# Low parts of 32 weight units by accumulating DMAs instead of VectorE

## The chip, the core and the metric

The kernel runs on one core of a Trainium2 chip. The metric is the device time of one execution in microseconds. The kernel before takes 855.59 us (median of 3 runs, 855.11 to 855.79).

The core has five engines with their own instruction queues, each worked off in order: TensorE (PE in the profile, with its weight loads as PEld), VectorE (DVE), ScalarE (ACT), GpSimd (POOL) and SyncE (SP). Sixteen DMA engines move data between memory and the on-chip SBUF.

## The reference

One decoder block on 512 tokens of width 1024, in float32. Two branches work on the same normed input and are merged by sigmoid gates; then come a squared-ReLU MLP of width 4096 and gated embeddings.

```
h = rms_norm(x, attn_norm_g);  u = h @ w_in                  # 1024 x 5376
u_sb, u_rw, u_gate = split(u)
o_sb = stick_breaking_attention(q, k, v of u_sb)             # 8 heads of 64
o_rw = rwkv7_time_mix(u_rw, ...)                             # 8 heads of 64, a recurrence over the tokens
g_sb, g_rw = sigmoid(u_gate)
x = x + (g_sb * (o_sb @ w_up_sb) + g_rw * (o_rw @ w_up_rw)) @ w_out
x = x + relu(rms_norm(x) @ w_ff1)**2 @ w_ff2
x = rms_norm(x + sigmoid(rms_norm(x) @ w_ple_gate) * (p @ w_ple_proj))
```

The recurrence of the RWKV branch, per head: S = S diag(w) + (S a) b^T + v k^T, y = S r.

## The kernel before

**Products in three parts.** TensorE multiplies in a format with a shorter mantissa (float32r). To keep float32's accuracy, every operand is split in a high part (the value rounded to float32r) and a low part (the value minus the high part), and a product is made of three matmuls: high by high (L244), low of the data by high of the weight (L245), high by low of the weight (L246). `mm3` issues the three; a weight unit is 128 x 1024 numbers (512 KB), eight `mm3` steps, 24 matmuls.

**Weight units.** All weights lie in memory as such units, and the list `seq` names them in the order of use: twelve of q, k and v, then (U_RW, 12) and (U_RW, 13), then the r, k and v projections of the four RWKV head pairs (U_RW, 0 to 11, three for each head pair), the gates (U_GSB and U_GRW, eight each), the two upward projections (U_UPSB and U_UPRW, four each), and the units of the later products. SyncE loads a unit to `w_raw` (L182, four buffers). `fetch_to` splits it: ScalarE casts it to `w_hi` (L225), VectorE writes `w_lo`, raw minus high (L227); `w_hi` and `w_lo` have three buffers each. `weights` hands a unit out. A unit's split is issued three `mm3` steps into the unit two places ahead of it, so it is to be ready some 1.6 units of matmuls later.

**Stages.** In the profile's time: to about 140 us the projections of q, k, v and the attention, with the last projections of that stage (among them (U_RW, 4), (U_RW, 0) and (U_RW, 8)) between its matmuls; from 140 to about 410 us the RWKV stage; then the merge and the product with `w_out`, then the MLP from about 480 us, and the gated embeddings at the end.

**The RWKV stage.** The four head pairs go through `prepare` and `scan`, one head pair's `scan` beside the next one's `prepare`. `prepare` builds operands for chunks of 64 tokens and inverts triangular matrices: on VectorE LM and DE (L852, L855), own (L888), the transposes LX (L899), tmp (L893), then seven pairs of X steps (L910, L911), own and X (L912, L915), with small matmuls on TensorE in between (L847, L901, L877, L937, L945, L956, L967). `scan` walks over the chunks: TensorE L996, VectorE UV (L998), TensorE L1005, VectorE S (L1013), which takes in Sg, made on GpSimd (L1012). Between these, as filling, stand the matmuls of the weight units above: their results leave PSUM by VectorE (u at L357, gg at L738). At the start of the stage ScalarE makes eight sigmoids (L682), a table load (L686), gx (L755) and further operands; GpSimd issues two accumulating DMAs (L635) which sum blocks of `w_out` to T3 and, after that has landed, T2.

**What sets the order.** The code is written as generators that `drive` interleaves, and a scheduler then sets the order of each engine's queue by its own reckoning of when each instruction can start; so a change of one instruction moves others. Waits are on semaphores. GpSimd issues the accumulating DMAs itself; one of them stands in its queue like any other instruction and waits there for its inputs.

Of the kernel before, what the change touches and what calls it, by code (L numbers as in the profile page):

```python
# [13 lines left out]
AF = mybir.ActivationFunctionType  # L14
ALU = mybir.AluOpType
# [25 lines left out]
U_PLE, U_QKV, U_RW, U_GSB, U_GRW, U_UPSB, U_UPRW, U_OUT, U_FF1, U_FF2, U_GATE = range(11)  # L41
# [52 lines left out]
def tile_block(ctx: ExitStack, tc: tile.TileContext, xT, xt, pT, wts, lora, cols_d, gfin_d, consts_d, out, dbg=None):  # L94
    nc = tc.nc
    act, dve, pool, pe, sync = nc.scalar, nc.vector, nc.gpsimd, nc.tensor, nc.sync
# [3 lines left out]
    def r32(ap):  # L100
        return ap.bitcast(F32)
# [34 lines left out]
    seq = []  # L136
# [24 lines left out]
    state = {"i": 0, "used": 0, "due": 0}  # L161
    AHEAD = 3
    homes = {}
# [3 lines left out]
    def unit(i):  # L167
        if seq[i][0] == U_FF2:
            return wts[UBASE[U_FF2] + seq[i][1] * 8 + FF2_FROM[seq[i][2]] + seq[i][3]]
        if seq[i][0] == U_S12:  # L170
            return wts[UBASE[U_FF1] + seq[i][1] * 8 + seq[i][2] + 4]
        if seq[i][1] == "s":
            return wts[UBASE[seq[i][0]] + FROM[seq[i][2]]]
        return wts[UBASE[seq[i][0]] + seq[i][1]]

    def load_to(n):
        while len(loaded) < min(n, len(seq)):
            i = len(loaded)
            loaded.append(None)
            if seq[i] not in sources and seq[i][0] not in (U_S3, U_S4):  # L180
                loaded[i] = wpool.tile([P, 1024], F32, name="w_raw", bufs=4)
                sync.dma_start(out=loaded[i], in_=unit(i))  # L182
                if seq[i][0] == U_FF2 and seq[i][2] == 3:
                    pool.dma_start(out=loaded[i], in_=wts[UBASE[U_FF2] + seq[i][1] * 8 + 4 + seq[i][3]], accum_op=ALU.add)
# [11 lines left out]
    def made(i):  # L196
        kind = seq[i][0]
        if seq[i] in sources:
            return sources[seq[i]]()
        if kind == U_S12:  # L200
            with tc.issue_after(state["wlo"]):
                four_sums(i)
            return sums12[seq[i][1:]][:, 0:2].rearrange("p s x -> p (s x)")
        if kind == U_S3:
            return loaded[i - 1]
        if kind == U_S4:
            return sums12.pop(seq[i][1:])[:, 2]
        return loaded[i]

    def fetch_to(n, ahead=0):  # L210
        while state["i"] < min(n, len(seq)):
            i = state["i"]
            state["i"] += 1
            load_to(i + 1 + ahead)
            raw = made(i)
            if seq[i] in homes:
                hi, lo = homes[seq[i]]()
            elif seq[i][0] == U_S4:
                hi = wpool.tile([P, 512], F32R, name="w_hi4", bufs=1)
                lo = wpool.tile([P, 512], F32R, name="w_lo4", bufs=1)  # L220
            else:
                hi = wpool.tile([P, 1024], F32R, name="w_hi")
                lo = wpool.tile([P, 1024], F32R, name="w_lo")
            with tc.issue_after(state["hx"] if seq[i] == (U_FF1, 4) else state["fourth"][0]) if seq[i] in ((U_FF1, 4), (U_OUT, 2), (U_OUT, 3)) else nullcontext():
                state["cast"] = act.copy(out=hi, in_=raw).ins  # L225
            with tc.issue_after(state["fourth"][1]) if seq[i] in homes and seq[i][0] == U_OUT else nullcontext():
                state["wlo"] = dve.tensor_tensor(out=lo, in0=raw, in1=r32(hi), op=ALU.subtract).ins  # L227
            if seq[i] == (U_OUT, "s", 4):
                state["fourth"] = state["cast"], state["wlo"]
            ready.setdefault(seq[i], []).append((hi, lo))  # L230

    def weights(*u):
        assert seq[state["used"]] == u, (seq[state["used"]], u)
        state["used"] += 1
        fetch_to(state["used"])
        state["due"] = 3
        return ready[u].pop(0)
# [11 lines left out]
    def step():  # L249
        state["due"] -= 1  # L250
        if state["due"] == 0:
            fetch_to(state["used"] + AHEAD - 1, 1)
# [77 lines left out]
    with ExitStack() as sA:  # L330
# [43 lines left out]
        with ExitStack() as s1:  # L374
# [47 lines left out]
            for i in range(2):  # L422
                ready[seq[i]] = [tuple(first_w[i])]
            fetch_to(3)

            for k in range(KT):
# [1262 lines left out]
```

## Time and profile before

| | |
|---|---|
| median of 3 runs | 855.59 us |
| profiled execution | 859.3 us, span 857.5 us |
| granted TensorE clock | 0.996 of full speed |
| busy: PE, DVE, ACT, POOL | 98%, 83%, 60%, 12% of the span |
| HBM read, written | 108.08 MB, 10.49 MB |

The span runs from the first to the last instruction of the profiled execution; its own device time is 1.8 us longer. "Busy" is the time in which an engine worked on an instruction. In rows of groups, `L227 DVE TENSOR_TENSOR w_lo<-w_raw,w_hi` is line 227 of the kernel before on VectorE, writing `w_lo` from `w_raw` and `w_hi`; after the shapes and the count stand the busy us, the mean ns of one, and the idle time of the engine ahead of them with what ended it. In rows of single instructions the start (us from the span's start) and the duration come first.

### The profile page before, as it was taken

Reading aid. Unit: us, or ns where it says so; the run is one execution under the profiler, and the core shown is the slowest. Engines: PE = TensorE matmul, PEld = TensorE weight load, DVE = VectorE, ACT = ScalarE, POOL = GpSimd, SP = SyncE. Lnnn points to the kernel's source line nnn. Section 1 sums busy time; section 2 is a strip of 40 time slices with the busy share of each in tenths; the row PEclk is TensorE's granted clock in tenths of the full one; section 3 lists DMA queues with packets and bytes.
Section 4 is the critical chain, followed back from the end, with each engine's and each line's share of the span. In section 5 each row is a group of like instructions: output and inputs, shape, how many; then the busy total and the mean of one; then the engine's idle time right before and its main releaser. Section 6 shows DMA issues by size and latency. Waiting matters only on the chain.

```text
span 857.5 us, 14647 instructions
## 1 busy us (share of the span) xinstructions
PE 840.8 (98%) x5594; PEld 697.5 (81%) x5594; DVE 712.6 (83%) x1264; ACT 513.1 (60%) x804; POOL 105.5 (12%) x174
## 2 busy tenths in 40 slices
PE   8999999999999999999999999999999999999996
PEld 5778788777777777777888888899889989988885
DVE  7989987896987969867896597899879988997767
ACT  7878887734436243533585575458647844783843
POOL 1332432001212101020000101000110010010000
PEclk9999999999999999999999999999999999999999
DMA  8311213421220323427882676973985489275402
GB/s 320 101 50 62 87 62 135 123 96 54 63 88 25 103 83 115 162 97 232 284 258 95 189 228 156 232 202 102 227 234 150 139 240 241 96 221 145 174 23 99
DMA packets 40197, 124.23 MB, mean 145 GB/s; under 512 B 4544, under 2 KB 4544, under 8 KB 40128
## 3 DMA queue, kind: packets, MB, share of 16 engines
q1 hardware_dynamic: 34944, 104.42, 35.7%
q0 software_dynamic: 5184, 18.88, 12.1%
q8 instruction: 44, 0.72, 0.4%
q14 instruction: 25, 0.20, 0.1%
HBM read 108.08 MB, written 10.49 MB: 138 GB/s over the span
## 4 chain that ended last, share of the span: by engine, by line
PE 87%; DVE 9%; issue 1%; ACT 1%; DMA 1%; SPq 0%; DVEq 0%; ACTq 0%
PE ps_m L244 14%; PE ps_m L245 14%; PE ps_m L246 14%; PE ps_m L260 9%; PE ps_m L259 9%; PE ps_m L261 9%; PE ps_g L877 1%; DVE w_lo L227 1%; PE ps_o L550 1%; PE ps_s L1005 1%; PE ps_z L558 1%; PE ps_c L996 1%; PE ps_g L967 1%; DVE LX L899 1%; DVE own L888 1%
## 5 line engine op out<-in xcount | busy, mean ns | idle before, releaser
L225 ACT CAST w_hi<-w_raw 128x1024 fp32r<-128x1024 f32 x122 | 128.0, 1051 | 122.4 <-PE ps_m L245 77.4
L227 DVE TENSOR_TENSOR w_lo<-w_raw,w_hi 128x1024 fp32r<-128x1024 f32 x122 | 149.0, 1224 | 24.2 <-ACT w_hi L225 23.5
L244 PE MATMUL ps_m<-h_hi,w_hi 128*128 128x512 f32 x320 | 130.6, 410 | 0.8 <-ACT w_hi L274 0.7
L246 PE MATMUL ps_m<-h_hi,w_lo 128*128 128x512 f32 x320 | 128.6, 402 | 0.0
L245 PE MATMUL ps_m<-h_lo,w_hi 128*128 128x512 f32 x320 | 128.2, 401 | 0.3 <-DVE h_lo L407 0.3
L244 PEld LDWEIGHTS ps_m<-h_hi,w_hi 128*128 128x128 f32 x320 | 60.7, 190 | 12.6 <-ACT w_hi L274 1.1
L246 PEld LDWEIGHTS ps_m<-h_hi,w_lo 128*128 128x128 f32 x320 | 60.4, 189 | 12.0
L245 PEld LDWEIGHTS ps_m<-h_lo,w_hi 128*128 128x128 f32 x320 | 60.5, 189 | 11.3 <-DVE h_lo L407 1.3
L245 PE MATMUL ps_m<-hx,w_hi 128*128 128x256 f32 (+1 forms) x208 | 65.8, 316 | 0.0
L244 PE MATMUL ps_m<-hx,w_hi 128*128 128x256 f32 (+1 forms) x208 | 65.8, 316 | 0.0
L246 PE MATMUL ps_m<-hx,w_lo 128*128 128x256 f32 (+1 forms) x208 | 65.7, 316 | 0.0
L244 PE MATMUL ps_m<-tb,w_hi 128*128 128x256 f32 x192 | 54.3, 283 | 0.0
L245 PE MATMUL ps_m<-tb,w_hi 128*128 128x256 f32 x192 | 54.3, 283 | 0.0
L246 PE MATMUL ps_m<-tb,w_lo 128*128 128x256 f32 x192 | 54.3, 283 | 0.0
L259 PE MATMUL ps_m<-w_hi,fS 128*128 128x512 f32 x128 | 49.8, 389 | 0.0
L260 PE MATMUL ps_m<-w_lo,fS 128*128 128x512 f32 x128 | 49.8, 389 | 0.0
L261 PE MATMUL ps_m<-w_hi,fS 128*128 128x512 f32 x128 | 49.8, 389 | 0.0
L245 PEld LDWEIGHTS ps_m<-hx,w_hi 128*128 128x128 f32 x208 | 39.6, 191 | 3.0 <-DVE hx L1158 0.4
L244 PEld LDWEIGHTS ps_m<-hx,w_hi 128*128 128x128 f32 x208 | 39.6, 191 | 2.8 <-ACT hx L1157 0.2
L246 PEld LDWEIGHTS ps_m<-hx,w_lo 128*128 128x128 f32 x208 | 39.6, 191 | 2.5
L259 PE MATMUL ps_m<-w_hi,fA 128*128 128x512 f32 x96 | 37.4, 389 | 0.0
L260 PE MATMUL ps_m<-w_lo,fA 128*128 128x512 f32 x96 | 37.4, 389 | 0.0
(425 smaller groups left out, 2147.2 us busy)
## 6 DMA issues: line engine op xcount, KB each, us to landing
w_raw<-in_wts_dram SPq DMA_DIRECT2D x129, 512.0 KB, 4.0
gates<-gg SPq DMA_DIRECT2D x16, 256.0 KB, 2.0
w_raw<-in_wts_dram POOLq DMA_DIRECT2D x8, 512.0 KB, 6.6
x_in<-in_xT_dram SPq DMA_DIRECT2D x8, 256.0 KB, 5.5
gb<-gates SPq DMA_DIRECT2D x8, 256.0 KB, 4.5
tmp<-gates SPq DMA_DIRECT2D x8, 256.0 KB, 2.9
upsb<-tmp SPq DMA_DIRECT2D x8, 256.0 KB, 5.1
ga<-upsb SPq DMA_DIRECT2D x8, 256.0 KB, 6.2
```

What stands on the lines that cost most here:

```text
L225: state["cast"] = act.copy(out=hi, in_=raw).ins
L227: state["wlo"] = dve.tensor_tensor(out=lo, in0=raw, in1=r32(hi), op=ALU.subtract).ins
L244: pe.matmul(ps, wh, xh[:, k, t], start=first, stop=False, skip_group_check=skip)
L245: pe.matmul(ps, wh, xl[:, k, t], start=False, stop=False, skip_group_check=skip)
L246: pe.matmul(ps, wl, xh[:, k, t], start=False, stop=last, skip_group_check=skip)
L259: pe.matmul(ps, xh[:, k + j], wh, start=first and j == 0, stop=False, skip_group_check=True)
L260: pe.matmul(ps, xh[:, k + j], wl, start=False, stop=False, skip_group_check=True)
L261: state["row"] = pe.matmul(ps, xl[:, k + j], wh, start=False, stop=last and j == 1, skip_group_check=True).ins
L550: pe.matmul(ps_o[:, j * P:T], vv[:, j, hh, :, :].rearrange("p a d -> p (a d)"), part[:, ZB[j]:ZB[j] + ZN[j]], start=j == 2 and part is wh, ...
L558: pe.matmul(zt[b][:, :n], tri, part[:, s:s + n], start=False, stop=False, skip_group_check=True)
L877: last = pe.matmul(ps[rows, k], left[rows, k, :], rhs[rows, k], start=True, stop=True)
L888: dve.tensor_tensor(out=own8[rows], in0=own, in1=b8[rows].broadcast_to([32, 8, 32]), op=ALU.mult)
```

## The change

For 32 units ((U_RW, 0) to (U_RW, 11), U_GSB, U_GRW and U_UPSB) VectorE's subtraction goes. ScalarE, after its cast to `w_hi`, writes minus the high part to `w_lo`, and GpSimd issues a DMA that reads the raw unit from memory a second time and adds it onto `w_lo`. The other units are split as before. Lines behind this place move by 7: L635 becomes L642, L246 becomes L253.

```
+    def by_dma(u):
+        return u[0] in (U_GSB, U_GRW, U_UPSB) or u[0] == U_RW and u[1] < 12
+
     def fetch_to(n, ahead=0):
...
                 state["cast"] = act.copy(out=hi, in_=raw).ins
-            with tc.issue_after(state["fourth"][1]) if seq[i] in homes and seq[i][0] == U_OUT else nullcontext():
-                state["wlo"] = dve.tensor_tensor(out=lo, in0=raw, in1=r32(hi), op=ALU.subtract).ins
+            if by_dma(seq[i]):
+                act.activation(out=lo, in_=r32(hi), func=AF.Copy, scale=-1.0)
+                pool.dma_start(out=lo, in_=unit(i), accum_op=ALU.add)
+            else:
+                with tc.issue_after(state["fourth"][1]) if seq[i] in homes and seq[i][0] == U_OUT else nullcontext():
+                    state["wlo"] = dve.tensor_tensor(out=lo, in0=raw, in1=r32(hi), op=ALU.subtract).ins
```

The scheduler orders the queues anew. Three places, before and after.

GpSimd at the start of the RWKV stage, before (L635 the two DMAs of T, T_1561 being T3 and T_1560 T2; L757 the copy gc):

```order
L753 MEMSET gx 128x8
L635 DMA T_1561<-in_wts_dram 128x1024
L635 DMA T_1560<-T_1561 128x1024
L757 COPY gc__1661<-gx 128x8
L753 MEMSET gx 128x8
L757 COPY gc__2168<-gx 128x8
L993 COPY UV<-UV_2098 64x128
```

The same place with the change (L231 the new accumulating DMA, L642 the DMAs of T, T_1566 being T3):

```order
L760 MEMSET gx 128x8
L231 DMA w_lo<-in_wts_dram 128x1024
L642 DMA T_1566<-in_wts_dram 128x1024
L642 DMA T_1565<-T_1566 128x1024
L764 COPY gc__1666<-gx 128x8
L231 DMA w_lo<-in_wts_dram 128x1024 x3
L760 MEMSET gx 128x8
L764 COPY gc__2178<-gx 128x8
L231 DMA w_lo<-in_wts_dram 128x1024 x4
```

The first L231 is that of (U_RW, 1), ahead of both DMAs of T; the three behind gc are (U_RW, 9), (U_GSB, 0) and (U_GSB, 1).

ScalarE at the same time, before (the last two of the eight sigmoids, then the first operands of `prepare`; L225 is the cast of (U_GSB, 0), that of (U_RW, 9) having come ahead of the sigmoids):

```order
L682 ACTIVATE w_1644<-ps_g,cols 128x512
L682 ACTIVATE a_1649<-ps_g,cols 128x512
L686 ACT_TABLE_LOAD
L755 ACTIVATE gx<-w_1611 128x8x64
L760 ACTIVATE tmp<-w_1611 128x512
L764 ACTIVATE tmp<-mix,cols 128x512
L225 CAST w_hi<-w_raw 128x1024
L697 CAST tmp<-tmp 128x512
L358 ACTIVATE mix<-u,omm 128x512
```

With the change (L230 the new copy with scale -1, the first of (U_RW, 9), the second of (U_GSB, 0); L228 the cast of (U_GSB, 0)):

```order
L689 ACTIVATE w_1649<-ps_g,cols 128x512
L689 ACTIVATE a_1654<-ps_g,cols 128x512
L693 ACT_TABLE_LOAD
L762 ACTIVATE gx<-w_1616 128x8x64
L767 ACTIVATE tmp<-w_1616 128x512
L771 ACTIVATE tmp<-mix,cols 128x512
L230 ACTIVATE w_lo<-w_hi 128x1024
L704 CAST tmp<-tmp 128x512
L365 ACTIVATE mix<-u,omm 128x512
L228 CAST w_hi<-w_raw 128x1024
L230 ACTIVATE w_lo<-w_hi 128x1024
```

The copy of (U_RW, 9) stands where the cast of (U_GSB, 0) stood, and that cast comes three instructions later.

VectorE in the third head pair's inverse, before (the last X steps):

```order
L910 TENSOR_TENSOR own_3022<-ps_g,X_3023 128x8
L227 TENSOR_TENSOR w_lo<-w_raw,w_hi 128x1024
L911 TENSOR_TENSOR X_3023<-X_3023,own_3022 128x8
L738 TENSOR_TENSOR gg<-ps_m,rs 128x512
L912 TENSOR_TENSOR own_3022<-X_3023,cst 128x256
L227 TENSOR_TENSOR w_lo<-w_raw,w_hi 128x1024
L915 STREAM_TRANSPOSE LX<-own_3022 128x8x32
```

With the change:

```order
L917 TENSOR_TENSOR own_3040<-ps_g,X_3041 128x8x2
L806 TENSOR_TENSOR Q<-mix,gx 128x4x64
L918 TENSOR_TENSOR X_3041<-X_3041,own_3040 128x8x2
L917 TENSOR_TENSOR own_3040<-ps_g,X_3041 128x8
L918 TENSOR_TENSOR X_3041<-X_3041,own_3040 128x8
L919 TENSOR_TENSOR own_3040<-X_3041,cst 128x256
L922 STREAM_TRANSPOSE LX<-own_3040 128x8x32
```

Two subtractions and the evacuation gg no longer stand between the last steps of the inverse.

## The prediction

> **What bounds the kernel now.** I read the busy times by stretches of the span, then the waits of TensorE, then the chain of work that ended last. The change touches 32 weight units whose low parts are made between about 85 and 410 us of the span, so these stretches matter. Columns: stretch, its length, then busy us (and instructions) of PE, PEld, DVE, ACT and POOL, granted clock, DMA share, GB/s.
>
> ```profile
> 85.00:140.00 55.00, 54.12 (x276) 44.06 (x275) 49.15 (x90) 44.96 (x81) 15.59 (x25) 1.00 0.20 68
> 140.00:410.00 270.00, 265.15 (x2474) 205.54 (x2473) 217.44 (x495) 123.49 (x197) 36.91 (x73) 0.99 0.35 111
> ...
> 137.00:170.00 33.00, 32.97 (x146) 26.48 (x145) 25.52 (x34) 24.70 (x38) 5.95 (x17) 1.00 0.53 151
> ```
>
> TensorE is busy 265.15 of the 270 us of the RWKV stage, VectorE 217.44. TensorE is idle 4.85 us there and 0.88 us between 85 and 140. Whatever VectorE gains can shorten the span only where TensorE waits. The waits of TensorE between 140 and 410 us (us in total, times, longest) say for whom:
>
> ```profile
> PE ps_g L937 <- issue: 1.4, 1, 1.4
> PE ps_s L1005 <- DVE UV L998: 0.8, 2, 0.4
> PE ps_g L901 <- DVE tmp L893: 0.7, 2, 0.6
> PE ps_c L996 <- DVE S L1013: 0.5, 1, 0.5
> ...
> PE ps_g L877 <- DVE own L912: 0.3, 1, 0.3
> PE ps_g L847 <- DVE DE L855: 0.2, 1, 0.2
> ```
>
> About 2.5 us of waiting is for VectorE, 1.4 us for nothing the profile shows. The chain of waits has six low-part subtractions of converted units in it, in all 6.4 us; the first and the last of them:
>
> ```profile
> 180.68 1.18 DVE w_lo L227
> ...
> 390.94 1.13 DVE w_lo L227
> ```
>
> These six look like the gain, but the chain names the last releaser, not the idle time: TensorE had fill matmuls of the weight units to run meanwhile, and its own waits add up to less. So the stage is TensorE's, with VectorE a few tenths of a microsecond behind it at a few points.
>
> **The change part by part.** *Removed from VectorE:* 32 subtractions of 1.218 us, 39 us.
>
> ```profile
> L227 DVE TENSOR_TENSOR w_lo<-w_raw,w_hi 128x1024 fp32r<-128x1024 f32 x31 | 37.8, 1218 | 2.7 <-ACT w_hi L225 2.4
> ```
>
> Nearly all of it is hidden behind matmuls. What can come back is bounded above by the 4.85 us of idle time and below by nothing. I take the three waits of the triangular inverse (L901, L877, L847: 1.2 us), in whose VectorE queue the subtractions stood, and half of the two scan waits (L1005, L996: 0.65 us): a gain of 1.8 us.
>
> *Added to ScalarE:* 32 copies with scale -1 of the shape that L225 has; the nearest price is that cast.
>
> ```profile
> L225 ACT CAST w_hi<-w_raw 128x1024 fp32r<-128x1024 f32 x122 | 128.0, 1051 | 122.4 <-PE ps_m L245 77.4
> ```
>
> That is 33.6 us on an engine that is busy 168.5 of these 325 us. None of TensorE's waits in the stage is for ScalarE, so the cover holds. If it fails, a copy costs 1.05 us where the next ScalarE result is awaited; two such places would be 2.1 us. Bounds 0 to 2.1, taken 0.4.
>
> *Added to GpSimd:* 32 issues, and with each a wait for ScalarE's copy, behind which the scan's Sg products and the gx work queue. Such issues take 0.85 to 1.03 us (rows below); GpSimd is busy 52.5 of the 325 us. Bounds 0 to 1.3 us (the two scan waits once more), taken 0.
>
> *Added to the DMA engines:* 32 accumulating transfers of 512 KB.
>
> ```profile
> q1 hardware_dynamic: 34944, 104.42, 35.7%
> q0 software_dynamic: 5184, 18.88, 12.1%
> ```
>
> The accumulating queue moved 18.88 MB, 36 transfers, in 12.1% of 857.5 us, 2.9 us of all engines each; a plain 512 KB load takes 306 us / 199, some 1.5 us. Between 137 and 170 us the share is 0.53 already, and five more accumulates there add 14.4 of 33 us: about 0.97.
>
> *Where it hurts: the ninth RWKV unit.* The low part used to be ready 1.2 us after the cast. Now it is ready after a copy, an issue and a landing. The cast runs 11 us or more ahead of the first use of a low part (shortest: (U_GSB, 0), cast at 158.12, first use at 170.15), so the new path mostly fits. Not for unit (U_RW, 9). In ScalarE's new order its copy stands behind the eight sigmoids, the table load and three activations; in time, before:
>
> ```profile
> 154.30 0.73 ACT L682 ACTIVATE a<-ps_g,cols 128x512 f32<-128x512 f32 x1
> 155.05 1.28 ACT L686 ACT_TABLE_LOAD   x1
> 156.34 0.63 ACT L755 ACTIVATE gx<-w 128x512 f32<-128x512 f32 x1
> 156.88 0.62 ACT L760 ACTIVATE tmp<-w 128x512 f32<-128x512 f32 x1
> 157.40 0.71 ACT L764 ACTIVATE tmp<-mix,cols 128x512 f32<-128x512 f32 x1
> 158.12 1.05 ACT L225 CAST w_hi<-w_raw 128x1024 fp32r<-128x1024 f32 x1
> ```
>
> The copy takes the place of the cast at 158.12, a fill matmul later (one stands ahead of the last sigmoid's matmul now), 158.3, and ends at 159.4. Its DMA is in GpSimd's queue behind both DMAs of T and gc:
>
> ```profile
> 147.68 1.03 POOL L635 DMA_DIRECT2D T<-in_wts_dram  x1 [0.21 <-issue]
> 154.90 0.87 POOL L635 DMA_DIRECT2D T<-T  x1 [6.19 <-DMA T<-in_wts_dram]
> 157.04 0.45 POOL L757 COPY gc__1661<-gx 128x8 f32<-128x8 f32 x1 [1.27 <-ACT gx L755]
> ...
> 484.01 0.85 POOL L1430 DMA_DIRECT2D B12a<-in_wts_dram  x1 [54.19 <-DMA B11a<-in_wts_dram]
> 486.18 0.86 POOL L1430 DMA_DIRECT2D B12b<-in_wts_dram  x1 [1.31 <-DMA B12b<-in_wts_dram]
> 491.01 0.85 POOL L1431 DMA_DIRECT2D B11a<-B12a  x1 [3.98 <-DMA B12a<-in_wts_dram]
> 497.42 0.88 POOL L1431 DMA_DIRECT2D B11b<-B12b  x1 [5.55 <-DMA B12b<-in_wts_dram]
> ```
>
> T's first DMA alone lands 7.2 us after its issue (the second, which waits for it, starts at 154.90). With another accumulate in flight it is 11.2 us (486.18 to 497.42). Now (U_RW, 1)'s accumulate goes out just ahead of T's, so T's, at about 148.6, lands between 155.8 and 159.8; T's second DMA and gc follow, and (U_RW, 9)'s is issued at 159.4 to 161, beside T's second one. Landing 7.2 to 11.2 us later, middle 9.2: 168.6. TensorE reads the first low part of this unit in the first row (the 153rd L246 matmul), of the next, (U_GSB, 0), in the second, and of the last converted one, 25 units on, in the third:
>
> ```profile
> 164.71 0.39 PE L246 MATMUL ps_m<-h_hi,w_lo 128*128 128x512 f32 x1
> ...
> 170.15 0.39 PE L246 MATMUL ps_m<-h_hi,w_lo 128*128 128x512 f32 x1
> ...
> 402.59 0.39 PE L246 MATMUL ps_g<-osb,w_lo 128*128 128x512 f32 x1
> ```
>
> Its place in TensorE's queue has not moved, and everything behind it waits: 168.6 - 164.7 = 3.9, say 4.0 us. Bounds: a landing as short as the shortest here (4.7 us) gives 164.1 and no stall; issue at 161 and 11.2 us give 172.2 and 7.5 us.
>
> ```profile
> DMA to landing us min/median/max: 4.7/5.8/6.9
> ```
>
> For (U_GSB, 0) ScalarE adds 0.62, 0.72, 1.05 and 1.05 us after 159.4, so its accumulate goes out at 162.9 and lands, 11.2 us later, at 174.1; its first use has by then moved to 170.15 + 4.0 = 174.2. One stall covers both.
>
> *Two rules of the skill.* The Trainium skill, DMA: Bandwidth & Descriptors, section Anatomy of one DMA — SWDGE (gpsimd) path, fits 2.0 us plus bytes over 436 GB/s; for 512 KB that is an estimate of 3.2 us, and by it the low part would land at 162.6, there would be no stall, and the sum would be -1.4 us. The rows, 7.2 and 11.2 us, do not bear it out for accumulates. The Trainium skill, SBUF — State Buffer, section on the "DVE blocks DMA" trap, says that descriptor writing for such a DMA is locked out while VectorE runs a two-port copy. That would speak against this change; the rows do not show it, since the issues beside a busy VectorE take 0.85 to 0.88 us.
>
> **Sum.** -1.8 (VectorE) + 4.0 (late low part) + 0.4 (ScalarE) = +2.6 us. Against the profiled execution: span 857.5 plus 2.6 is 860.1, 861.9 with the 1.8 us that lay around it (859.3 - 857.5). The median of the runs, 855.59, is 3.7 below that execution; the same difference on it gives 858.2 us.
>
> **The rivals.** *A, the forecast:* one low part lands late and TensorE stands; 858.2, its own range 857.3 to 861. For it: the queue positions and the landings. Against it: a landing under 6 us. *B, no measurable change:* the stall is short (7.2 us from 159.4 is 166.6, 1.9 us) and VectorE's gain of 1.8 pays for it: 855.6 - 1.8 + 1.9 + 0.4 = 856.1. The skill's short landing (854.2) belongs here too. *C, faster:* it turns on TensorE's idle time. If VectorE's queue is what caused it all, and the 1.4 us without a releaser goes too, TensorE gets back 4.0 of its 4.85 us and the low part lands in time: 851.6. For it: six subtractions in the chain. Against it: the waits themselves, 2.5 us. It wins if accumulates land under about 6 us. *D, DMA engines full:* with a share near 1 between 137 and 170 us, and 0.54 plus five or six accumulates (17 us of 43) from 367 on, raw loads and low parts both slip; two more units late by the same 4 us: 866. It decides where a unit takes 5.4 us of TensorE (164.71 to 170.15) and its two transfers 4.4 us of the DMA engines. That pace holds only around 165 us; over the 25 units up to 402.59 it is 232.4 / 25 = 9.3 us.
>
> ```profile
> 367.00:410.00 43.00, 42.84 (x230) 33.26 (x229) 29.25 (x62) 16.19 (x25) 5.58 (x13) 1.00 0.54 173
> ```
>
> **How the numbers follow.** A 0.44, B 0.27, C 0.21, D 0.08. What a measurement of this kernel can tell from no change is 0.2%, 1.7 us: 853.9 to 857.3. A and D are slower (0.52), B is the same (0.27), C faster (0.21). The range leaves out the outer half of C and of D: 852.0 to 863.5 us.
>
> **What would show it.** Right: in the waits of TensorE a row L253 waiting for DMA into w_lo, several us long, near 165 us of the span, and hardly any elsewhere; VectorE's busy time down by 39 us and ScalarE's up by 33 in the stage; TensorE's waits for VectorE halved; GpSimd's issue for that unit at 159 to 161. Wrong: no DMA among TensorE's waits (then C or B), or such waits spread over many units (D), or waits for ScalarE in their place. The gain is right if the span between 170 and 410 us, counted from the same matmul, is 1 to 3 us shorter. A shorter span by 4 us or more would mean that the busy time of TensorE hid waits that I read as work.

## The result, and the profile after

The changed kernel takes 877.25 us (median of 6 runs) against 855.53 us for the kernel before in the same job: 1.0252 times as long, 95% interval 1.021 to 1.0293. One of the six runs, at 887.45 us, was in a slower state of the chip and is left out of this ratio; the median of the other five is 876.75 us. The forecast was 858.2 us, so the sign was right and the size was not: 21.7 us in place of 2.6. The profiled execution took 877.75 us, its span is 875.9 us, 18.4 us longer than that of before. The traces differ by less than the medians because the profiled execution of before lies 3.7 us above its median.

The stretches of the changed kernel (same columns as in the prediction):

```profile
137.00:170.00 33.00, 28.82 (x118) 22.59 (x116) 17.68 (x25) 27.87 (x39) 8.95 (x20) 0.95 0.78 182
140.00:410.00 270.00, 258.41 (x2425) 200.62 (x2424) 180.66 (x459) 145.38 (x218) 63.02 (x102) 0.97 0.63 149
```

VectorE has what the change promised it: 180.66 us of work between 140 and 410 us where it had 217.44. TensorE lost by it: 258.41 busy us where it had 265.15, at a granted clock of 0.97. The DMA engines went from a share of 0.35 to 0.63.

The DMA queues of the changed kernel (packets, MB, share of 16 engines over the span):

```profile
q1 hardware_dynamic: 34944, 104.42, 34.8%
q0 software_dynamic: 9792, 35.66, 23.2%
```

The accumulating queue grew from 12.1% of 857.5 us (104 us) to 23.2% of 875.9 us (203 us): 3.1 us of all engines for each of the 32 transfers. The forecast had 2.9.

The waits of TensorE between 85 and 490 us, the changed kernel (us in total, times, longest; all over 1 us):

```profile
PE ps_m L253 <- DMA w_lo<-in_wts_dram: 3.7, 1, 3.7
PE ps_m L266 <- ACT ps_m L1124: 2.9, 1, 2.9
PE ps_g L686 <- ACT lx L678: 2.2, 2, 1.1
PE ps_m L251 <- issue: 1.9, 1, 1.9
PE ps_g L944 <- DVE LX L934: 1.6, 1, 1.6
```

The first row is the stall of the forecast, 3.7 us where it had 4.0, at the place it named. The other four rows were not foreseen. All rows of this view add up to 15.7 us; the same view of before adds up to 5.3.

The rest is clock. Two stretches of the changed kernel beside that first wait, the stand itself and what follows it:

```profile
167.80:171.20 3.40, 0.18 (x1) 0.00 (x0) 3.23 (x7) 2.90 (x4) 0.86 (x1) 1.00 1.03 246
171.30:174.60 3.30, 2.94 (x7) 2.36 (x8) 3.30 (x6) 1.27 (x2) 0.59 (x2) 0.50 1.02 259
```

TensorE does next to nothing for 3.4 us, and then works at a granted clock of 0.50. The trace's clock records show five such stretches between 85 and 480 us, three of 3.41 us and two of 6.83 us, each in or right behind one of the stands above; before there was one of 3.41 us. That is up to (23.9 - 3.4) / 2 = 10.2 us. Waits that grew by 10.4 us and a clock that cost up to 10.2 us, less where half clock fell on idle time, make the 18.4 us. All of it is lost before 480 us: from there to the end the same matmul comes 18.4 us later than before.

### The profile page after: what moved, and what is told of

Same layout as the page of the kernel before. It is cut to its first block, busy times and chain, and to the rows that moved or that the text cites. A ratio compares the mean times of both kernels' runs of the same rounds, so it can differ in the third digit from the quotient of the medians.

```text
span 875.9 us, 14711 instructions
## 1 busy us (share of the span) xinstructions
PE 848.3 (97%) x5594; PEld 703.2 (80%) x5594; DVE 678.3 (77%) x1232; ACT 543.4 (62%) x836; POOL 134.6 (15%) x206
## 3 DMA queue, kind: packets, MB, share of 16 engines
q0 software_dynamic: 9792, 35.66, 23.2%
## 4 chain that ended last, share of the span: by engine, by line
PE 47%; DVE 2%; ACT 1%; DMA 1%; issue 0%; ACTq 0%
PE ps_m L266 9%; PE ps_m L267 9%; PE ps_m L268 9%; PE ps_m L252 6%; PE ps_m L253 6%; PE ps_m L251 6%; PE ps_m L1160 1%; DMA gb<-gates 1%; DVE hx L1165 0%; DVE xs L1542 0%; DVE t L1541 0%; DVE sums L1144 0%; DVE hx L282 0%; DVE r L308 0%; DVE r L309 0%
## 5 line engine op out<-in xcount | busy, mean ns | idle before, releaser
L228 ACT CAST w_hi<-w_raw 128x1024 fp32r<-128x1024 f32 x122 | 127.7, 1049 | 105.1 <-PE ps_m L252 66.4
L251 PE MATMUL ps_m<-h_hi,w_hi 128*128 128x512 f32 x320 | 132.6, 416 | 2.9 <-issue 1.9
L253 PE MATMUL ps_m<-h_hi,w_lo 128*128 128x512 f32 x320 | 130.2, 407 | 3.7 <-DMA w_lo<-in_wts_dram 3.7
L234 DVE TENSOR_TENSOR w_lo<-w_raw,w_hi 128x1024 fp32r<-128x1024 f32 x90 | 109.9, 1226 | 30.0 <-ACT w_hi L228 29.7
L253 PEld LDWEIGHTS ps_m<-h_hi,w_lo 128*128 128x128 f32 x320 | 61.1, 191 | 16.3 <-DMA w_lo<-in_wts_dram 4.1
L253 PE MATMUL ps_m<-hx,w_lo 128*128 128x256 f32 (+1 forms) x208 | 65.7, 316 | 0.0
L253 PE MATMUL ps_m<-tb,w_lo 128*128 128x256 f32 x192 | 54.3, 283 | 0.0
L266 PE MATMUL ps_m<-w_hi,fS 128*128 128x512 f32 x128 | 49.8, 389 | 0.0
L231 POOL DMA_DIRECT2D w_lo<-in_wts_dram x32 | 28.5, 891 | 129.1 <-ACT w_lo L230 128.8
L253 PEld LDWEIGHTS ps_m<-hx,w_lo 128*128 128x128 f32 x208 | 39.6, 191 | 2.5
L266 PE MATMUL ps_m<-w_hi,fA 128*128 128x512 f32 x96 | 37.4, 389 | 0.0
```

The lines of the kernel that those rows point to most:

```text
L231: pool.dma_start(out=lo, in_=unit(i), accum_op=ALU.add)
L251: pe.matmul(ps, wh, xh[:, k, t], start=first, stop=False, skip_group_check=skip)
L253: pe.matmul(ps, wl, xh[:, k, t], start=False, stop=last, skip_group_check=skip)
L266: pe.matmul(ps, xh[:, k + j], wh, start=first and j == 0, stop=False, skip_group_check=True)
```

## The experiments

Each time below is set against the kernel before as it ran on the same chip in the same job. "Share" is the time in units of that. The rows e3, e6 to e10, e12 and e15_late4 rest on four runs, the others on five to ten.

| kernel | us | share (95%) | against before |
|---|---|---|---|
| the change | 877.25 | 1.0252 (1.021 to 1.0293) | +21.7 |
| e2: without its DMAs | 854.28 | 0.998 (0.997 to 0.999) | -1.7 |
| e8: its DMAs to a spare tile | 878.75 | 1.025 (1.0201 to 1.03) | +22.8 |
| e3: before, plus DMAs to a spare tile | 871.72 | 1.018 (1.0131 to 1.0229) | +15.8 |
| e7: plain loads from GpSimd | 865.82 | 1.0108 (1.0089 to 1.0128) | +9.9 |
| e10: accumulates from `w_raw` | 865.9 | 1.0104 (1.0076 to 1.0133) | +9.8 |
| e5: head, 8 units | 859.67 | 1.0047 (1.0033 to 1.0061) | +3.7 |
| e4: middle, 12 units | 856.82 | 1.0007 (0.9994 to 1.002) | +0.9 |
| e6: tail, 12 units | 869.74 | 1.0157 (1.0142 to 1.0172) | +13.8 |
| e12: U_GRW, 8 units of the tail | 866.14 | 1.0107 (1.0079 to 1.0135) | +10.0 |
| e13: U_UPSB, 4 units of the tail | 860.04 | 1.0042 (1.0029 to 1.0055) | +3.9 |
| e11: middle, from `w_raw` | 854.68 | 0.9983 (0.9972 to 0.9995) | -1.4 |
| e16: middle and 5 more, from `w_raw` | 856.73 | 1.0013 (1.0003 to 1.0022) | +1.2 |
| e9: GpSimd subtracts | 907.1 | 1.0602 (1.0586 to 1.0617) | +51.5 |
| e15_late3 | 856.61 | 1.0001 (0.9989 to 1.0014) | +1.0 |
| e15_late4 | 859.85 | 1.004 (1.0025 to 1.0055) | +4.3 |

Line numbers behind `fetch_to` differ by up to four between these kernels.

### Without the DMAs (e2)

```
                 act.activation(out=lo, in_=r32(hi), func=AF.Copy, scale=-1.0)
-                pool.dma_start(out=lo, in_=unit(i), accum_op=ALU.add)
```

> The changed kernel without its 32 DMAs: ScalarE writes minus the high part, and nothing is added to it, so the low parts are left wrong. The order of the queues of TensorE, VectorE, ScalarE and SyncE is that of the changed kernel, row by row. Theory T (the transfers load the DMA engines, so that other transfers land later and TensorE stands): back to 852 to 857 us. Theory L (TensorE waits for the landing of its own low parts, my prediction's one): the same, 852 to 857. Theory O (the new order of the queues, with ScalarE's copies in it, costs the time): 870 to 877 us, as with the change.

Measured: 854.28 us, 0.998 of before. The waits of TensorE between 85 and 480 us in this kernel, the three longest:

```profile
PE ps_s L1011 <- DVE UV L1004: 0.8, 2, 0.4
PE ps_g L943 <- DVE LX L933: 0.7, 1, 0.7
PE ps_g L980 <- ACT W L975: 0.6, 1, 0.6
```

Nothing is left of the four long rows, and no half clock in the stage. So theory O falls: the new order of the queues, ScalarE's 33.8 us of copies and VectorE's relief together are worth -1.7 us, where the forecast had -1.8 for VectorE and +0.4 for ScalarE. The whole loss hangs on the DMAs; whether by their own landing or by what they do to others, this run can't tell.

### The same transfers, nobody waiting for them (e8, e3)

```
...
+                pool.tensor_copy(out=r32(state["dump"])[:, 0:1], in_=r32(lo)[:, 0:1])
-                pool.dma_start(out=lo, in_=unit(i), accum_op=ALU.add)
+                pool.dma_start(out=state["dump"], in_=unit(i), accum_op=ALU.add)
```

> The changed kernel's order, but each of the 32 accumulating DMAs goes to a spare tile that nobody reads; low parts are left as minus the high part, so they are wrong. TensorE waits for no landing of a low part, but the same bytes move at about the same times (one copy of 128 x 1 on GpSimd ties each issue to ScalarE's copy; a DMA to the spare tile waits for the one before it). T: 870 to 878 us, with the waits of TensorE at 148, 301, 358 and 445 us still there. L: 853 to 858. O: 870 to 877, with or without transfers.

The lines left out make the spare tile, `dump`, and set it to zero once; it shares its memory with two small tiles of the MLP that are used from 560 us on. e3 has the two added lines behind VectorE's subtraction, which stays as it was before.

> The kernel before, with VectorE's subtractions and the same order of the queues of TensorE, VectorE, ScalarE and SyncE, plus the 32 accumulating DMAs into a spare tile that nobody reads. T: 866 to 878 us, and transfers such as those of gates and tmp take 1.5 to 2 times as long as before. L and O: no change, 854 to 858 us.

Measured: 878.75 and 871.72 us. The first rows of TensorE's waits between 85 and 480 us in e8:

```profile
PE ps_g L985 <- ACT W L980: 3.8, 1, 3.8
PE ps_m L255 <- issue: 2.7, 1, 2.7
PE ps_g L690 <- ACT lx L682: 2.4, 2, 1.4
```

TensorE waits for no low part there, and the time is the changed kernel's. In e3 even VectorE's work and the old order are in place, and the 32 transfers that nobody reads cost 15.8 us. Theory L, the one of the forecast, falls as the main cause; theory T holds: the transfers hurt others. As T expected of e3, the transfers of the gates took longer: `gates<-gg` a median of 3.3 us where it had 2.0, `tmp<-gates` 4.2 where it had 2.9. Two reservations. With a single spare tile, 11 of e8's transfers waited for the one before at the head of GpSimd's queue, so its bursts are less dense than the change's; that the scan was held up by this doesn't show in e3, where TensorE's two waits in the scan are those of before (0.8 and 0.5 us). And the size of e3 is known roughly: its four runs lie at 867.6, 868.7, 874.8 and 876.3 us. The same traffic costs 24.5 us in the new order (878.75 - 854.28) and 15.8 in the old one; the intervals of e8's and e3's shares overlap, and whether the order makes a difference stays open.

### What the transfers delay

The traces show chains through transfers that have nothing to do with the change.

*At 148 us.* The attention's last store (o_sb) must land before the RWKV stage may use its memory. ScalarE there, before:

```profile
144.13 0.61 ACT L668 CAST lw<-lora_w 64x512 fp32r<-64x512 f32 x1
...
145.27 1.25 ACT L671 CAST lx<-t 64x512 fp32r<-64x512 f32 x2
```

ScalarE and GpSimd with the change:

```profile
146.06 0.62 ACT L675 CAST lw<-lora_w 64x512 fp32r<-64x512 f32 x1 [2.29 <-DMA o_sb<-oo]
...
147.21 1.05 ACT L230 ACTIVATE w_lo<-w_hi 128x1024 fp32r<-128x1024 f32 x1
148.16 1.24 ACT L678 CAST lx<-t 64x512 fp32r<-64x512 f32 x2
```
```profile
139.71 0.86 POOL L231 DMA_DIRECT2D w_lo<-in_wts_dram  x1 [5.92 <-ACT w_lo L230]
```

The store went out at 140.8 us as before, but 1.1 us behind an accumulate, and landed after 5.2 us where it took 2.9. lw came 1.9 us later, lx 2.9 us, since one of the new copies (L230) also stands ahead of it, and TensorE stood twice for 1.1 us at L686. The store alone is enough for that: e2 has the copy and no such stand, e3 has no copy, its store took 6.5 us, and the two stands are there (2.0 us together).

*From 340 us on.* The gated products read the gates back from memory, and SyncE and ScalarE, each working its queue in order, wait for these transfers. The stores of the gates, `gates<-gg`, took a median of 3.5 us from issue to landing with the change and 2.0 before, the reloads `tmp<-gates` 4.2 and 2.9. e6 below shows such a wait at its full length. In the changed kernel the reload issued at 350.8 us took 5.5 us; ScalarE's work on it and its copy of y followed, and VectorE, which reads y, came late to the LX that TensorE's L944 waited for (1.6 us):

```profile
358.21 0.69 DVE L1044 TENSOR_REDUCE st<-y 128x8 f32<-128x512 f32 x1 [1.89 <-ACT y L1034]
...
360.01 0.42 DVE L934 TENSOR_TENSOR LX<-ps_g,LX 128x256 f32<-128x256 f32 x1
```

At 400 us the queue of SyncE waits for a landing, with the change:

```profile
399.78 0.32 SPq L740 DMA_DIRECT2D upsb<-tmp  x1
407.07 0.32 SPq L732 DMA_DIRECT2D tmp<-gates  x1
```

and the same two rows before:

```profile
387.70 0.32 SPq L733 DMA_DIRECT2D upsb<-tmp  x1
390.53 0.32 SPq L725 DMA_DIRECT2D tmp<-gates  x1
```

The second transfer needs the first one's buffer. That one landed after 7.3 us beside the accumulate issued at 398.46 us, and after 2.8 us before. The queue falls 4.5 us back there, and the merge behind it: its load of the gates (`gb<-gates`) that went out at 412.8 us before goes out at 430.0, 17.2 later, while TensorE's matmuls of that time are some 11 us later. TensorE's stand at L266, at 447 us, comes 36 us after the last accumulate landed. That it follows from this lag fits the times, but I have not followed it link by link; in e6, with the tail's transfers alone, it is 0.9 us and not 2.9.

*At 302 us* TensorE waits for "issue"; the last section shows what I take that for.

### Where the loss lies (e5, e4, e6, e12, e13)

```
     def by_dma(u):
-        return u[0] in (U_GSB, U_GRW, U_UPSB) or u[0] == U_RW and u[1] < 12
+        return u[0] in (U_GRW, U_UPSB)
```

(e6; the others name their units in the same place.)

> The change for the first 8 of the 32 units only ((U_RW, 4, 0, 8, 5, 1, 9), (U_GSB, 0, 1)), whose transfers run between about 113 and 178 us. Theory T (the added transfers crowd out others): with the change TensorE lost some 8 to 9 us more than before between 137 and 180 us, at 148 us (behind the late landing of the attention's last store) and at 167 us (the low part of (U_RW, 9)), each with a window of half clock behind it; so 861 to 867 us. If the loss were a matter of the whole load or of the order of the queues, 8 of 32 units would cost a quarter, about 861 or less; 856 if there is none here.

> The change for 12 of the 32 units only, those used between about 188 and 292 us, where the DMA engines were busy 0.20 to 0.25 of the time before. T: there is room for the transfers, so 853 to 858 us; a little of VectorE's gain may show. L: the landings of 5.4 to 7.2 us fit in the lead of 8 us or more, 853 to 858. O: the order costs 12/32 of the loss, about 863 us.

> The change for the last 12 units only (U_GRW, U_UPSB), whose transfers run between about 310 and 411 us. T: with the change TensorE lost 9 us more than before between 314 and 480 us, most of it at 443 to 450, long after the last accumulate; so 862 to 868 us, with the waits at 440 to 450 us still there. If those waits belong to the head's delay and not to the tail's transfers, 855 to 858 us.

> The change for U_GRW alone, 8 of the 12 units of the tail, transfers between about 310 and 390 us. The tail as a whole cost 13.4 us more than before. If the loss goes with the number of units: +9 us, 864 to 866. If it is the transfers beside the stores and loads of the gated products (tmp, upsb, ga, gb from 385 us on): 856 to 860 us here, and the larger part with U_UPSB.

> The change for U_UPSB alone, 4 units, transfers between about 383 and 410 us, where the DMA engines were busy more than half of the time before. By number of units: +4.5 us, 859 to 861. If the crowd at 385 to 410 us is what matters: 863 to 868 us.

Measured: +3.7, +0.9 (not told from 0), +13.8, +10.0 and +3.9 us. Head, middle and tail add up to 18.4 of the 21.7; U_GRW and U_UPSB add up to the tail. My expectation for the head was too high (861 to 867 us, measured 859.67), that for the tail too low (862 to 868, measured 869.74), and the tail's loss doesn't stand where I had put it: TensorE's wait at 443 us in e6 is 0.9 us. Of the two rules that I had offered for the tail, the number of units holds, 1.25 us for each in U_GRW and 1.0 in U_UPSB, and the crowd at 385 to 410 us does not. The number doesn't hold outside: the middle's 12 units cost nearly nothing. Each of these kernels has its own order of the queues; only that of the whole change was tried by itself (e2).

A chain of the tail, ScalarE in e6:

```profile
364.62 0.59 ACT L965 COPY MA<-ps_g 128x512 f32<-128x512 f32 x1 [0.34 <-PE ps_g L963]
369.56 0.63 ACT L734 ACTIVATE tmp<-tmp 128x512 f32<-128x512 f32 x1 [4.36 <-DMA tmp<-gates]
370.10 0.35 ACT L976 COPY W<-ps_g 128x256 f32<-128x256 f32 x1
```

and what TensorE waits for in e6, first rows:

```profile
PE ps_g L884 <- issue: 3.1, 1, 3.1
PE ps_g L981 <- ACT W L976: 2.9, 1, 2.9
PE ps_m L252 <- issue: 2.3, 1, 2.3
```

ScalarE stands for 4.36 us at the head of its queue for gates that it reads back, and W, which TensorE's L981 needs, is queued behind it: 2.9 us. The two "issue" rows are more, 5.4 us together, and two of the three stretches of half clock in e6 follow them; the last section is about such waits. In the middle no chain through the gates runs: they are only written there. The DMA engines have room too, a share of 0.53 in e4 between 188 and 292 us, where it was 0.19 before.

### What makes a transfer dear (e7, e10)

```
-                pool.dma_start(out=lo, in_=unit(i), accum_op=ALU.add)
+                pool.dma_start(out=lo, in_=unit(i))                          # e7
+                pool.dma_start(out=lo, in_=raw, accum_op=ALU.add)            # e10
```

> The changed kernel in the same order of all five queues, but its 32 DMAs only load the unit over the low part and add nothing, so the low parts are wrong. Theory T1 (an accumulate costs the DMA engines about twice a plain load of the same bytes, 2.9 to 3.1 us against 1.5 us by the rows): the loss falls by half or more, 858 to 867 us. Theory T2 (it is the bytes read from memory, or the landing from GpSimd's queue, accumulate or not): 873 to 878 us.

> The change with one word different: the accumulating DMAs read the raw unit where it already lies on the chip (w_raw), not from memory a second time. TensorE's and VectorE's orders are those of the changed kernel; a w_raw buffer comes free only when its accumulate has landed. Theory T3 (the price is the accumulate in the DMA engines, whatever its source): 870 to 880 us. Theory T4 (the price is the second read from memory): 856 to 864 us.

Measured: 865.82 and 865.9 us. The queue's share in e7, then in e10:

```profile
q0 software_dynamic: 9792, 35.66, 18.9%
```
```profile
q0 software_dynamic: 9792, 35.66, 22.0%
```

Less the 104 us of before, a plain load takes 1.9 us of all engines (18.9% of 865.1 us), an accumulate from the chip 2.7 (22.0% of 865.3), one from memory 3.1. Against the kernel without DMAs (-1.7 us) these three cost 11.6, 11.5 and 23.4 us. So T1 holds, half the loss is the accumulate. For e10 the time lies between the ranges of T3 and T4: leaving out the second read halves the loss, though the engines' time falls by an eighth only. Occupied time alone doesn't set the price. The landings rank as the losses do, medians of 4.7, 4.8 and 6.4 us, but that they set the price isn't shown. In e10 the raw buffers also come free later, which this run doesn't separate.

### A version that beats both (e11, e16, e9)

> The same, for the middle 12 units alone, which cost nothing that could be measured when they were read from memory (ratio 1.0007). T3: 855.5 to 857.5 us. T4: a part of VectorE's gain comes through, 853.5 to 855.5 us.

> The accumulates from w_raw for the middle 12 units, which ran at 0.9983 of the time before, and for five more: (U_RW, 4), (U_RW, 0), (U_GRW, 0, 1, 2), whose transfers fall between 113 and 125 and between 310 and 330 us. If room in the DMA engines decides: 853.5 to 855.5 us. If (U_RW, 0)'s transfer beside the attention's last store, or U_GRW's beside the loads of the gates, holds something up again: 857 to 861.

> For the same 32 units GpSimd subtracts (low part = raw - high part) in place of VectorE; no DMA, no copy on ScalarE. The subtraction of 128 x 256 on GpSimd took 0.87 us before, so one of 128 x 1024 about 3.5 us, 112 us on an engine that had 272 of 325 us free. If the gain of an unburdened VectorE is what the kernel without DMAs showed (854.3 us) and GpSimd's products for the scan are not held up: 853.5 to 855.5 us, faster than before. If the scan waits behind the subtractions in GpSimd's queue: 857 to 865 us.

e11, the middle's 12 units accumulated from `w_raw`, takes 854.68 us, 0.9983 of the time before (0.9972 to 0.9995): 1.4 us less than before, a gain that is just clear of the noise, and some 23 less than the change. That is T4's range. Its transfers as the page lists them:

```profile
w_lo<-w_raw POOLq DMA_DIRECT2D x12, 512.0 KB, 4.4
```

Five units more (e16) give it back: +1.2 us, between the two ranges that I had expected. GpSimd's own subtraction (e9) is far slower, 907.1 us, outside both of my ranges. One took 2.4 us, less than the 3.5 I had worked out, and GpSimd isn't the bound. The first waits of TensorE in e9, 85 to 490 us:

```profile
PE ps_c L1002 <- DVE S L1019: 9.4, 7, 3.0
PE ps_g L708 <- DVE tmp L704: 5.9, 4, 2.1
```

TensorE waits for VectorE there, in the scan above all. VectorE hardly waited for GpSimd's scan products (3.9 us in all); it was slowed itself beside GpSimd. A subtraction on GpSimd in e9, an instruction of VectorE beside it, and the same instruction with none beside it:

```profile
167.84 2.37 POOL L230 TENSOR_TENSOR w_lo<-w_raw,w_hi 128x1024 fp32r<-128x1024 f32 x1 [1.89 <-ACT w_hi L228]
```
```profile
168.38 2.38 DVE L704 TENSOR_TENSOR tmp<-tmp 128x512 fp32r<-128x512 f32 x1 [0.80 <-ACT tmp L703]
...
186.11 0.68 DVE L704 TENSOR_TENSOR tmp<-tmp 128x512 fp32r<-128x512 f32 x1
```

An estimate from this trace: the instructions of VectorE that ran mostly beside one of these subtractions, each less the median of the same instruction elsewhere in e9, add up to some 44 us, near the 51.5 that the kernel lost. Those that read one operand from PSUM were not slowed (the UV of the scan took 0.28 us either way).

### What one stand costs (e15)

The kernel without DMAs, with (U_RW, 9)'s low part made late on GpSimd (3 or 4 times):

```
+                for _ in range(4 if seq[i] == (U_RW, 9) else 0):
+                    pool.tensor_tensor(out=lo, in0=r32(lo), in1=r32(lo), op=ALU.add)
```

> The kernel without the 32 DMAs (854.3 us, low parts left wrong), in the same order of TensorE, VectorE, ScalarE and SyncE, with one low part made late by hand: GpSimd adds (U_RW, 9)'s low part to itself three times, 2.4 us each by the subtractions of the same shape. The low part is ready at 159.8 + 7.2 = 167.0 us, first use 165.1: a stand of 1.9 us and no other. If a stand costs its own length: 856.2 us. If a window of half clock (3.41 us long) follows, 1.7 us more: 857.9.

> The same with four additions: ready at 169.4, a stand of 4.3 us, the size of my prediction's one term. If it costs its own length: 858.6 us. With one window of half clock behind it 860.3, with two 862.0.

Measured: 856.61 and 859.85 us. The additions took 2.16 us each, not 2.4, so in e15_late3 the low part was ready just in time and its profile has no stand at that place, and in e15_late4 the stand is 1.9 us, not 4.3; the times can't be held against the expected ones. Nor was the low part the only thing made late: VectorE was slowed beside the additions, as in e9. In e15_late3:

```profile
158.88 1.91 DVE L706 TENSOR_TENSOR tmp<-tmp 128x512 fp32r<-128x512 f32 x1 [0.88 <-ACT tmp L705]
```

The same instruction took 0.69 us in e2, and TensorE waits 1.1 us for it, in both kernels of e15. In e15_late4 the wait for the low part, and the stretches up to 168.3 us and behind it:

```profile
PE ps_m L254 <- POOL w_lo L232: 1.9, 1, 1.9
```
```profile
164.90:168.30 3.40, 1.53 (x8) 0.95 (x6) 2.07 (x3) 3.14 (x5) 3.18 (x2) 1.00 0.00 0
168.40:171.70 3.30, 3.30 (x9) 2.53 (x9) 3.13 (x7) 2.42 (x4) 0.12 (x1) 0.50 0.41 159
```

A stand of 1.9 us, and behind it 3.41 us at half clock, 1.7 us more. Between the same two matmuls (the 145th and the 161st that reads a low part, counted as in the prediction) the traces of e2, e15_late3 and e15_late4 have 11.5, 12.95 and 16.47 us: the step from three additions to four is 3.5 us, the stand and its half clock (3.6) and not the stand alone. The two medians differ by 3.2 us.

## Why the prediction was wrong

**The bound** held: TensorE sets the stage, and the six subtractions in the chain were not worth their 6.4 us.

**VectorE, -1.8, and ScalarE, +0.4**: right as a sum, -1.7 us without the DMAs (e2) where the forecast had -1.4, and only in part as an account. In e2's trace the three waits of the inverse (1.2 us) are gone, as forecast, but the scan's two are whole (0.8 and 0.5 us), and two new waits stand there, 0.7 us for VectorE's LX and 0.6 for ScalarE's W. So the agreement has some luck in it; which waits make up the 1.7 us isn't shown. "The cover holds" for ScalarE was read from a trace in which ScalarE's own transfers landed in time. In the changed kernel the rows L686 and L266, 5.1 us, are waits for ScalarE.

**GpSimd, 0**: right as far as seen. The issues took 0.86 to 1.05 us, and no wait of TensorE hangs on its queue alone. It did stand 10.4 us for T's first DMA, which took 11.3 us where it had 6.9, but the issue for (U_RW, 9), at 162.82 us, came only 0.4 us behind ScalarE's copy.

**The late low part of (U_RW, 9), +4.0**: right in place, and in size by luck, since errors cancelled. The copy ended at 162.5 us, not 159.4, since the whole stage was late by then; the landing took 8.8 us, not 9.2; and the first use had itself moved from 164.71 to about 168. In e5, with the same transfers up to this place, more half clock had come before it, the landing took 5.4 us, and the wait is 0.3 us. By the fit in the Trainium skill, DMA: Bandwidth & Descriptors, section Anatomy of one DMA — SWDGE (gpsimd) path, 512 KB would land in 3.2 us, an estimate. Here plain loads from GpSimd landed after a median of 4.7 us and accumulates after 6.4, so the sum by that section of the Trainium skill (-1.4 us) was further off than the rows. And the stand of 3.7 us brought 1.7 us of half clock with it, a price that the sum left out, although the one drop of the clock in the trace of before lay right behind the one wait of 1.4 us.

**The step that failed** is the term that isn't in the sum: "*Added to the DMA engines:* 32 accumulating transfers of 512 KB". I worked out that each takes 2.9 us of all engines and that the share at 137 to 170 us would rise to 0.97 (it was 0.78), and then charged nothing for it but the landing of the low part itself. What else was in flight, stores and reloads for which SyncE, ScalarE and GpSimd wait at the head of in-order queues, had no row in my sum. The runs give this term some 15.8 us with the old order (e3) and 24.5 in the order of the change (e8 against e2), in both with nobody waiting for a low part; the change as a whole lost 23.4 us against e2.

**Rival D** named that resource, with a chance of 0.08 and 866 us. Its rule, that the transfers matter only where a unit's two transfers take as long as its matmuls, was wrong: between 314 and 367 us the share was 0.67 in the changed kernel, not 1, and a third of the engines' time free on average did not keep a 256 KB transfer from taking twice or three times as long beside an accumulate. The dense places were right, though: head and tail cost, the middle doesn't. **Rival B** is what the middle units alone do (856.82), and **C** (851.6) was beyond what the empty DMA queue gave (854.28).

**The signs that I named** did part of their work. The L253 row stands near 165 us, at 168 to 171.7, and nowhere else; yet half of the added waiting is for ScalarE, which I had listed as a sign against the forecast. Others were off too: TensorE's waits for VectorE between 140 and 410 us were not halved (3.3 us, from 2.7), the issue for (U_RW, 9) came at 162.8, not 159 to 161, and the same matmul at the end of the stage was 2.1 us later, counted from 170 us, not 1 to 3 earlier. I had looked for lateness in the rows that the change touches; it was in rows that it doesn't.

## What to carry to other kernels

Price a transfer by what it delays, not by its own landing: list the transfers that are in flight beside it, and ask which engine waits for each of them at the head of its queue, and what is queued behind. In this kernel an accumulate cost as much as two loads, and half of that was saved by adding from the chip instead of from memory; the place where it paid was the one where nothing waited for a transfer. Before work goes to GpSimd, ask what VectorE does beside it. And when TensorE stands for about 2 us, add 1.7 us for the clock: here most such stands had it.

## What the runs showed that I had not expected

**Half clock behind short stands.** In the profiles of all kernels here but e9, TensorE stood 24 times for 1.55 us or more between 85 and 490 us; 21 of these had 3.41 or 6.83 us at a granted clock of 0.5 beginning in them or within 3 us of their end. Single stands of 0.9 to 1.45 us were not, with one exception, the 1.4 us at 305 us of the kernel before; but two of 1.1 us, two microseconds apart, were enough. The Trainium skill, TensorE: Matmul & The Clock Gate, section Part 1: The HAM clock gate (the "warmup" mystery), describes a free-running window of 3413 ns, and the lengths agree with that. The same page of the Trainium skill, section Why this matters for your kernels, asks for no idle gaps over some 3 us; here 1.6 to 2.3 us were mostly too long already.

**"Issue" waits come with instruction loads.** TensorE's waits without a releaser, over 0.5 us, were 12 in the profiles of before, the change, e2 to e8 and e9 (e2 has none); in each case one 16 KB packet of the queue "instruction" had begun some 2.2 to 2.6 us before TensorE went on. The five in e10, e11, e12 and e16 (1.0 to 2.2 us) are the same. In e6, TensorE, then the queues between 299.5 and 300.6 us:

```profile
298.05 0.76 PE L884 MATMUL ps_g<-LX,LB 32*32 32x64 f32 x40
301.88 0.54 PE L884 MATMUL ps_g<-LX,LB 32*32 32x64 f32 x24 [3.08 <-issue]
```
```profile
q8 instruction: 1, 0.02, 5.5%
```

The packet began at 299.56 us and TensorE went on at 301.88, in the middle of a burst of small matmuls. These waits were up to 1.4 us before and up to 3.1 us with accumulates. That they are waits for instructions, and that accumulates delay those loads too, fits these rows; no run tried it by itself.
